# A decode step in which the sample group's local-attention caches are loaded two sequences at a time, 128 rows each

## The chip, the cores and the metric

The kernel runs on one core of one Trainium2 chip. Its engines work from queues of their own: TensorE (PE, with its weight loads PEld), VectorE (DVE), ScalarE (ACT), GpSimd (POOL) and SyncE (SP), which here only issues DMAs. The metric is the device time of one execution in microseconds (us), as the median of several runs. A result within 0.2% of the time before, about 5 us, counts as no change.

## What is computed

One layer of a hybrid decoder for a prompt group (one sequence of 256 tokens) and a sample group (8 sequences, one new token each) that share the weights: a half-step FFN, a mixer (gated DeltaNet beside sliding-window attention), cross-attention to a memory of 256 tokens, another half-step FFN, a final norm. The change lies in the sliding-window attention of the sample group:

```python
def swa_sample(q, k, v, sinks, k_buf, v_buf):        # k_buf, v_buf: (8, 128, 4, 64), oldest first
    kk = jnp.concatenate([k_buf, k], 1)              # 129 rows a sequence
    vv = jnp.concatenate([v_buf, v], 1)
    s = jnp.einsum('bthgd,bkhd->bhgtk', qg, kk) * (D ** -0.5)
    rel = (jnp.arange(T)[:, None] + wb) - jnp.arange(wb + T)[None, :]
    s = jnp.where((rel >= 0) & (rel < WINDOW), s, -jnp.inf)
    p = sink_softmax(s, sinks)
    o = jnp.einsum('bhgtk,bkhd->bthgd', p, vv)
    return o, kk[:, -wb:], vv[:, -wb:]
```

With a window of 128 and 128 cached rows, row 0 (the oldest) is masked out, so that 128 rows count: cache rows 1 to 127 and the new token. The order of these rows among themselves changes no sum, as long as keys and values have the same order. Each sequence has 4 key heads of 64, so that a row is 256 floats, 1 KB. All is in 32-bit floats.

## The kernel before

Nearly all of the time are large matrix products. `gemm` streams a weight matrix in pieces of 512 floats x 256 columns (`raw`, 512 KB, four buffers, loaded on SP at L152), splits each on ACT (`wh`, L155) and DVE (`wl`, L156) into two parts, and multiplies by 264 columns (256 prompt tokens and 8 sample tokens) in three products per 128 x 128 block (L183 to L185). Rows with `mm` or `mx` as output are these products. All smaller work runs in between.

The program is written in stages (the function `mixer`, printed below), and a scheduler then orders each engine's instructions by a simulated time, so that the stages overlap. `c0` to `c3` are pairs of DeltaNet heads (outputs `gd`), `s` projects keys, values and queries for the sliding window, `w0` to `w3` are the prompt's attention and `x` is the sample group's (outputs `sw`). The gate products (L900) fill TensorE meanwhile; their results go to DRAM from POOL (`gd<-gt`, L904), through two buffers.

In the stage `x` (`swa_sample`, written as a loop over 8 sequences) a sequence's keys come into a buffer `kc` by two DMAs on SP: rows 1 to 127 of its cache (L850), and the new key from the tile `kn` as row 127 (L851). TensorE transposes the block (L854), ACT copies it from PSUM (`kcT`, L856), and TensorE multiplies it by the queries (`qb`, L858). After a softmax the values come in the same way (L882, and L883 from `vn`) and are multiplied at L886. `kc` has two buffers for the keys and values of all sequences.

SP issues in order: a DMA that waits for its buffer, or that is slow to be issued, holds back the weight pieces and the state loads (`T`, `U`, `bv`, `d`, L658) behind it. At L682 TensorE multiplies the DeltaNet states by 2 columns, 32 instructions in a row per pair of heads. At L739 the rotary embedding swaps half-heads by DMAs on SP (`cth<-cy`).

Of the kernel before, what the change touches and what calls it, by code (L numbers as in the profile page):

```python
# [6 lines left out]
F32 = mybir.dt.float32  # L7
# [8 lines left out]
P = 128  # L16
# [3 lines left out]
NS = 8  # L20
# [49 lines left out]
class Build:  # L70
# [652 lines left out]
    def swa_proj(self, win, xs):  # L723
        nc, mc, o, i = self.nc, self.mc, self.o, self.i
        idn = self.K(C_ID)
        TT = nc.vector.tensor_tensor
        self.qr = mc.tile([P, 8, TOK], F32, name="qr")
        self.kd = {}
        self.Vt = mc.tile([P, 2, 256], F32, name="Vt")
        self.vn = mc.tile([NS, 256], F32, name="vn")  # L730
        self.kn = mc.tile([NS, 256], F32, name="kn")
        kt = mc.tile([P, 256], F32, name="kt")

        def rope_in(ps):
            y = self.gp.tile([P, TOK], F32, name="cy", bufs=2)
            TT(out=y, in0=ps, in1=self.norm.finish(), op=ALU.mult)
            t = mc.tile([P, TOK], F32, name="cth", bufs=2)
            for r in range(0, P, 32):
                nc.sync.dma_start(out=t[r:r + 32], in_=y[r ^ 32:(r ^ 32) + 32])  # L739
            TT(out=t, in0=t, in1=self.K(C_SN, TOK), op=ALU.mult)  # L740
            TT(out=y, in0=y, in1=self.K(C_CS, TOK), op=ALU.mult)
            return y, t

        def ev_k(j, ps):
            y, t = rope_in(ps)
            for par in range(2):
                g = 2 * j + par
                kd = mc.tile([P, TOK], F32, name=f"kd{g}")
                src = slice(64 * par, 64 * par + 64)
                for half in range(2):  # L750
                    TT(out=kd[64 * half:64 * half + 64], in0=y[src], in1=t[src], op=ALU.add)
                self.kd[g] = kd
                pt = self.evt()
                nc.tensor.transpose(pt[:, 0:64], kd[0:64, P:NP], idn[0:64, 0:64])
                nc.tensor.transpose(pt[0:NS, 64:128], kd[0:64, NP:TOK], idn[0:64, 0:64])
                nc.scalar.copy(out=kt[:, g * 64:(g + 1) * 64], in_=pt[:, 0:64])
                nc.scalar.copy(out=self.kn[:, g * 64:(g + 1) * 64], in_=pt[0:NS, 64:128])

        def ev_v(j, ps):
            y = self.gp.tile([P, TOK], F32, name="cy", bufs=2)  # L760
            TT(out=y, in0=ps, in1=self.norm.finish(), op=ALU.mult)
            pt = self.evt()
            nc.tensor.transpose(pt[:, 0:P], y[:, 0:P], idn)
            nc.tensor.transpose(pt[:, P:2 * P], y[:, P:NP], idn)
            nc.tensor.transpose(pt[0:NS, 256:384], y[:, NP:TOK], idn)
            nc.scalar.copy(out=self.Vt[:, :, j * P:(j + 1) * P], in_=pt[:, 0:256].rearrange("p (a b) -> p a b", a=2))
            nc.scalar.copy(out=self.vn[:, j * P:(j + 1) * P], in_=pt[0:NS, 256:384])

        def ev_q(c, ps):
            y, t = rope_in(ps)  # L770
            TT(out=self.qr[:, c], in0=y, in1=t, op=ALU.add)

        self.gemm(win, OFF_K, 256, xs, ev_k)
        self.gemm(win, OFF_V, 256, xs, ev_v)
        nc.gpsimd.dma_start(out=o["k_p"][0, 0].rearrange("t g d -> t (g d)"), in_=kt)
        ins = nc.gpsimd.dma_start(out=o["v_p"][0, 0].rearrange("t g d -> t (g d)"), in_=self.Vt[:, 1, :])
        with self.tc.issue_after(ins.ins):
            for nm, src, new in (("k_s", "cache_swa_k", self.kn), ("v_s", "cache_swa_v", self.vn)):
                nc.gpsimd.dma_start(out=o[nm][0, :, 0:P - 1], in_=i[src][0, :, 1:P])
                nc.gpsimd.dma_start(out=o[nm][0, :, P - 1].rearrange("b g d -> b (g d)"), in_=new)  # L780
            nc.gpsimd.dma_start(out=o["conv_s"][0, :, 0:2, :], in_=i["state_conv"][0, :, 1:3, :])
        for t0 in range(0, 8, 2):
            self.gemm(win, OFF_Q + t0 * P, 256, xs, lambda j, ps, t0=t0: ev_q(t0 + j, ps))

    def swt(self):
        return self.sw.tile([P, 512], F32, name="sw")
# [47 lines left out]
    def swa_sample(self):  # L834
        nc, mc, i, o = self.nc, self.mc, self.i, self.o
        idn = self.K(C_ID)
        TT = nc.vector.tensor_tensor
        sc = slice(NP, TOK)
        half = lambda q: slice(64 * q, 64 * q + 64)
        qb = mc.tile([P, NS, 2, 8], F32, name="qb")  # L840
        nc.vector.memset(qb, 0.0)
        for par in range(2):
            for jp in range(2):
                dst = qb.rearrange("p b t (r jj q) -> p r q t jj b", r=2, q=2)[half(par), par, jp]
                src = self.qr.rearrange("p (t r jj) x -> p r t jj x", t=2, r=2)[half(jp), par][:, :, :, sc]
                nc.vector.tensor_copy(out=dst, in_=src)
        ps = self.swt()
        for b in range(NS):
            kc = mc.tile([P, 256], F32, name="kc", bufs=2)
            nc.sync.dma_start(out=kc[0:P - 1], in_=i["cache_swa_k"][0, b, 1:P].rearrange("t g d -> t (g d)"))  # L850
            nc.sync.dma_start(out=kc[P - 1:P], in_=self.kn[b:b + 1, :])  # L851
            pt = self.swt()
            for t in range(2):
                nc.tensor.transpose(pt[:, t * P:(t + 1) * P], kc[:, t * P:(t + 1) * P], idn)  # L854
            kT = mc.tile([P, 2, P], F32, name="kcT", bufs=2)
            nc.scalar.copy(out=kT, in_=pt[:, 0:256].rearrange("p (a b) -> p a b", a=2))  # L856
            for t in range(2):
                nc.tensor.matmul(ps[:, b * 16 + t * 8:b * 16 + t * 8 + 8], kT[:, t], qb[:, b, t], start=True, stop=True)  # L858
        s1 = mc.tile([P, P], F32, name="s1")
        nc.vector.tensor_copy(out=s1, in_=ps[:, 0:P])  # L860
        pt = self.swt()
        nc.tensor.transpose(pt[:, 0:P], s1, idn)
        st = lambda name: mc.tile([P, 1], F32, name=name)
        m, se, sm = st("ssm"), st("sse"), st("ssu")
        nc.vector.tensor_reduce(out=m, in_=pt[:, 0:P], axis=AX.X, op=ALU.max)
        nc.vector.scalar_tensor_tensor(out=m, in0=m, scalar=0.125, in1=self.sinkc, op0=ALU.mult, op1=ALU.max)
        TT(out=se, in0=self.sinkc, in1=m, op=ALU.subtract)
        nc.vector.tensor_scalar(out=m, in0=m, scalar1=-1.0, scalar2=None, op0=ALU.mult)
        nc.scalar.activation(out=se, in_=se, func=AF.Exp)
        p = mc.tile([P, P], F32, name="s1")  # L870
        nc.scalar.activation(out=p, in_=pt[:, 0:P], func=AF.Exp, scale=0.125, bias=m, accum_out=sm)
        TT(out=sm, in0=sm, in1=se, op=ALU.add)
        nc.vector.reciprocal(out=sm, in_=sm)
        nc.vector.tensor_scalar(out=p, in0=p, scalar1=sm, scalar2=None, op0=ALU.mult)
        pt = self.swt()
        nc.tensor.transpose(pt[:, 0:P], p, idn)
        pT = mc.tile([P, P], F32, name="s3")
        nc.scalar.copy(out=pT, in_=pt[:, 0:P])
        po = self.swt()
        for b in range(NS):  # L880
            vc = mc.tile([P, 256], F32, name="kc", bufs=2)
            nc.sync.dma_start(out=vc[0:P - 1], in_=i["cache_swa_v"][0, b, 1:P].rearrange("t g d -> t (g d)"))  # L882
            nc.sync.dma_start(out=vc[P - 1:P], in_=self.vn[b:b + 1, :])  # L883
            for t in range(2):
                n = b * 16 + t * 8
                nc.tensor.matmul(po[:, n:n + 8], vc[:, t * P:(t + 1) * P], pT[:, n:n + 8], start=True, stop=True)  # L886
        for par in range(2):
            for jp in range(2):
                dst = self.os.rearrange("p (t r jj) x -> p r t jj x", t=2, r=2)[half(jp), par][:, :, :, sc]
                src = po[:, 0:P].rearrange("p (b t r jj q) -> p r q t jj b", b=NS, t=2, r=2, q=2)[half(par), par, jp]  # L890
                nc.vector.tensor_copy(out=dst, in_=src)
# [369 lines left out]
```

## Time and profile before

| | |
|---|---|
| median of 3 runs | 2570.62 us (2567.1 to 2571.18) |
| profiled execution, first to last instruction | 2570.9 us |
| TensorE busy | 2507.5 us, 98% |
| VectorE, ScalarE, GpSimd busy | 59%, 43%, 6% |
| bytes over DMA | 456.16 MB, mean 177 GB/s |

The profile gives the span of one execution; what lies around it can't be seen in the median, which is 0.3 us below the span. TensorE is busy nearly throughout, so the places to look at are those where it waits, and those where its granted clock is below 1. The granted clock takes two levels, 1.2 and 2.4 GHz, which the profile gives as 0.5 and 1.

### The profile page before, as it was taken

The page shows a single profiled execution, that of the slowest core. Times are in us where ns is not written, and L with a number is a line of the kernel's source. Part 1 is how long each engine was busy: PE and PEld are TensorE (multiplying, and loading weights), DVE is VectorE, ACT ScalarE, POOL GpSimd, SP SyncE. Part 2 cuts the span into 40 slices and gives each one's busy share as a digit, 9 for nine tenths or more (in the row PEclk, how much of TensorE's full clock was granted, in tenths as well). Part 3 has the DMA queues.
Part 4 walks back from the last instruction along what each step waited for, and adds up shares of the span by engine and source line. Part 5 has one row for each costly group of instructions (what it writes and reads, how often), then busy time and mean ns, then how long its engine had stood idle before and what let it go on. Part 6 is the DMA issues. An engine that isn't in the chain of part 4 may idle for free.

```text
span 2570.9 us, 48618 instructions
## 1 busy us (share of the span) xinstructions
PE 2507.5 (98%) x20127; PEld 2464.5 (96%) x20127; DVE 1508.5 (59%) x2507; ACT 1110.3 (43%) x1667; POOL 151.0 (6%) x203
## 2 busy tenths in 40 slices
PE   8999999999999999999789999999999999999998
PEld 8999999999998999989779999979999999999997
DVE  6555544555556858685355667687655544555544
ACT  4444333444444443454335545436444433444443
POOL 3000000000001002020020320000000000000000
PEclk9999999999999999999779999999999999999999
DMA  6555556556555556554345776674555555555553
GB/s 193 180 180 181 177 181 185 181 181 181 177 180 174 157 161 207 152 157 122 117 127 151 222 245 201 203 268 152 181 181 181 174 180 187 181 179 182 173 176 129
DMA packets 438589, 456.16 MB, mean 177 GB/s; under 512 B 18140, under 2 KB 425360, under 8 KB 438312
## 3 DMA queue, kind: packets, MB, share of 16 engines
q1 hardware_dynamic: 429376, 427.26, 53.9%
q0 software_dynamic: 8656, 24.67, 2.9%
q8 instruction: 157, 2.57, 0.4%
q10 hardware_dynamic: 336, 1.12, 0.1%
q14 instruction: 64, 0.52, 0.1%
HBM read 438.92 MB, written 14.98 MB: 177 GB/s over the span
## 4 chain that ended last, share of the span: by engine, by line
PE 93%; DMA 3%; DVE 2%; SPq 1%; ACT 0%; issue 0%; DVEq 0%; ACTq 0%
PE mm L183 18%; PE mm L185 18%; PE mm L184 18%; PE mx L183 11%; PE mx L185 11%; PE mx L184 11%; DMA kc<-kn 1%; DMA kc<-vn 1%; PE gd L574 1%; PE gd L579 1%; PE sw L803 1%; PE gd L682 1%; DVE wl L156 1%; DMA raw<-in_w_in_dram 0%; PE mm L988 0%; PE mm L990 0%
## 5 line engine op out<-in xcount | busy, mean ns | idle before, releaser
L156 DVE TENSOR_TENSOR wl<-raw,wh 128x1024 fp32r<-128x1024 f32 (+1 forms) x796 | 959.9, 1206 | 827.4 <-ACT wh L155 822.2
L155 ACT CAST wh<-raw 128x1024 fp32r<-128x1024 f32 (+1 forms) x796 | 820.5, 1031 | 1246.6 <-PE mm L184 669.1
L183 PE MATMUL mm<-xh,wh 128*128 128x264 f32 x2688 | 783.0, 292 | 6.0 <-ACT wh L155 6.0
L185 PE MATMUL mm<-xh,wl 128*128 128x264 f32 x2688 | 779.4, 291 | 3.4 <-DVE wl L156 3.4
L184 PE MATMUL mm<-xl,wh 128*128 128x264 f32 x2688 | 778.5, 290 | 0.0
L183 PEld LDWEIGHTS mm<-xh,wh 128*128 128x128 f32 x2688 | 518.4, 193 | 10.0 <-ACT wh L155 6.2
L185 PEld LDWEIGHTS mm<-xh,wl 128*128 128x128 f32 x2688 | 516.8, 193 | 6.4 <-DVE wl L156 4.2
L184 PEld LDWEIGHTS mm<-xl,wh 128*128 128x128 f32 x2688 | 517.7, 193 | 1.9 <-issue 1.5
L183 PE MATMUL mx<-xh,wh 128*128 128x264 f32 x1424 | 405.2, 285 | 1.1 <-DVE xl L1210 1.1
L185 PE MATMUL mx<-xh,wl 128*128 128x264 f32 x1424 | 405.4, 285 | 0.0
L184 PE MATMUL mx<-xl,wh 128*128 128x264 f32 x1424 | 404.4, 284 | 0.0
L183 PEld LDWEIGHTS mx<-xh,wh 128*128 128x128 f32 x1424 | 268.7, 189 | 1.4 <-issue 1.3
L184 PEld LDWEIGHTS mx<-xl,wh 128*128 128x128 f32 x1424 | 268.2, 188 | 0.0
L185 PEld LDWEIGHTS mx<-xh,wl 128*128 128x128 f32 x1424 | 268.1, 188 | 0.0
L185 PE MATMUL mm<-hh,wl 128*128 128x264 f32 x748 | 212.7, 286 | 0.0
L183 PE MATMUL mm<-hh,wh 128*128 128x264 f32 x748 | 212.4, 284 | 0.0
L184 PE MATMUL mm<-hl,wh 128*128 128x264 f32 x748 | 212.3, 284 | 0.0
L185 PE MATMUL mx<-hh,wl 128*128 128x264 f32 x660 | 187.6, 285 | 0.0
L183 PE MATMUL mx<-hh,wh 128*128 128x264 f32 x660 | 187.5, 284 | 0.0
L184 PE MATMUL mx<-hl,wh 128*128 128x264 f32 x660 | 187.4, 284 | 0.0
L184 PEld LDWEIGHTS mm<-hl,wh 128*128 128x128 f32 x748 | 140.9, 188 | 0.0
L183 PEld LDWEIGHTS mm<-hh,wh 128*128 128x128 f32 x748 | 140.6, 188 | 0.0
(572 smaller groups left out, 3020.9 us busy)
## 6 DMA issues: line engine op xcount, KB each, us to landing
raw<-in_ffn_w_dram SPq DMA_DIRECT2D x512, 512.0 KB
raw<-in_w_in_dram SPq DMA_DIRECT2D x152, 512.0 KB
raw<-in_w_out_dram SPq DMA_DIRECT2D x32, 512.0 KB
raw<-in_ffn_w_dram SPq DMA_DIRECT2D x32, 256.0 KB
raw<-in_w_br_gdn_dram SPq DMA_DIRECT2D x16, 512.0 KB
raw<-in_w_br_swa_dram SPq DMA_DIRECT2D x16, 512.0 KB
gd<-gt POOLq DMA_DIRECT2D x32, 132.0 KB, 3.2
tg<-gd POOLq DMA_DIRECT2D x32, 132.0 KB, 4.2
```

Source lines behind the costliest of these rows:

```text
L155: nc.scalar.copy(out=H, in_=raw)
L156: nc.vector.tensor_tensor(out=L, in0=raw, in1=H.bitcast(F32), op=ALU.subtract)
L183: nc.tensor.matmul(acc, wh, xh, start=(kg + c == 0), stop=False)
L184: nc.tensor.matmul(acc, wh, xl, start=False, stop=False)
L185: nc.tensor.matmul(acc, wl, xh, start=False, stop=(kg + c == nk - 1))
L574: nc.tensor.matmul(pP[:, a], A[:, a], uh[a], start=True, stop=True)
L579: nc.tensor.matmul(pU[:, a], T[:, a], Pm[:, a], start=True, stop=True)
L682: nc.tensor.matmul(pk[:, m:m + 2], Ss[h * 2 + b // 4][:, b % 4], kq[:, h, b, :], start=True, stop=True)
L803: nc.tensor.matmul(ps[j % 2][:, a // 2], self.qr[half, 2 * g + j // 2, qs], self.kd[g][half, 0:W], start=True, stop=True)
```

## The change

The keys and values of the sample group are loaded as whole blocks of two sequences, 128 rows x 2 x 256 (four loads for keys, L857, and four for values, L891, instead of eight each), on SP as before. The new token takes the place of row 0 and no longer of row 127. For keys this happens after the transposition: the new keys are taken already transposed from `kd` into a small tile `knT` (four DVE copies), and a DVE copy per sequence writes column 0 of `kcT` (L864); there is no DMA for it. For values a DMA per sequence writes row 0 of the block from `vn`, now issued by POOL (L893) and no longer by SP. `kc` has three buffers of two sequences each, and the prompt's key tile `kt`, which goes out as a cache, takes the first turn of one of them; the softmax's `s1`, `p` and `pT` use turns of `kcT`'s buffers; `kn` and `vn` lie in one tile.

```diff
@@ -727,9 +727,9 @@
         self.qr = mc.tile([P, 8, TOK], F32, name="qr")
         self.kd = {}
         self.Vt = mc.tile([P, 2, 256], F32, name="Vt")
-        self.vn = mc.tile([NS, 256], F32, name="vn")
-        self.kn = mc.tile([NS, 256], F32, name="kn")
-        kt = mc.tile([P, 256], F32, name="kt")
+        kvn = mc.tile([40, 256], F32, name="kvn")
+        self.kn, self.vn = kvn[0:NS], kvn[32:32 + NS]
+        kt = self.kc_tile()[:, 0, :]
...
@@ -781,6 +781,9 @@
             nc.gpsimd.dma_start(out=o["conv_s"][0, :, 0:2, :], in_=i["state_conv"][0, :, 1:3, :])
         for t0 in range(0, 8, 2):
             self.gemm(win, OFF_Q + t0 * P, 256, xs, lambda j, ps, t0=t0: ev_q(t0 + j, ps))
+
+    def kc_tile(self):
+        return self.mc.tile([P, 2, 256], F32, name="kc", bufs=3)
 
     def swt(self):
         return self.sw.tile([P, 512], F32, name="sw")
@@ -844,19 +847,25 @@
                 dst = qb.rearrange("p b t (r jj q) -> p r q t jj b", r=2, q=2)[half(par), par, jp]
                 src = self.qr.rearrange("p (t r jj) x -> p r t jj x", t=2, r=2)[half(jp), par][:, :, :, sc]
                 nc.vector.tensor_copy(out=dst, in_=src)
+        knT = mc.tile([P, 2, NS], F32, name="knT")
+        for t in range(2):
+            for q in range(2):
+                nc.vector.tensor_copy(out=knT[half(q), t, :], in_=self.kd[2 * t + q][half(q), sc])
         ps = self.swt()
-        for b in range(NS):
-            kc = mc.tile([P, 256], F32, name="kc", bufs=2)
-            nc.sync.dma_start(out=kc[0:P - 1], in_=i["cache_swa_k"][0, b, 1:P].rearrange("t g d -> t (g d)"))
-            nc.sync.dma_start(out=kc[P - 1:P], in_=self.kn[b:b + 1, :])
-            pt = self.swt()
-            for t in range(2):
-                nc.tensor.transpose(pt[:, t * P:(t + 1) * P], kc[:, t * P:(t + 1) * P], idn)
-            kT = mc.tile([P, 2, P], F32, name="kcT", bufs=2)
-            nc.scalar.copy(out=kT, in_=pt[:, 0:256].rearrange("p (a b) -> p a b", a=2))
-            for t in range(2):
-                nc.tensor.matmul(ps[:, b * 16 + t * 8:b * 16 + t * 8 + 8], kT[:, t], qb[:, b, t], start=True, stop=True)
-        s1 = mc.tile([P, P], F32, name="s1")
+        for b2 in range(0, NS, 2):
+            kc = self.kc_tile()
+            nc.sync.dma_start(out=kc, in_=i["cache_swa_k"][0, b2:b2 + 2].rearrange("b t g d -> t b (g d)"))
+            for b in (b2, b2 + 1):
+                pt = self.swt()
+                for t in range(2):
+                    nc.tensor.transpose(pt[:, t * P:(t + 1) * P], kc[:, b - b2, t * P:(t + 1) * P], idn)
+                kT = mc.tile([P, 2, P], F32, name="kcT", bufs=2)
+                nc.scalar.copy(out=kT, in_=pt[:, 0:256].rearrange("p (a b) -> p a b", a=2))
+                nc.vector.tensor_copy(out=kT[:, :, 0], in_=knT[:, :, b])
+                for t in range(2):
+                    nc.tensor.matmul(ps[:, b * 16 + t * 8:b * 16 + t * 8 + 8], kT[:, t], qb[:, b, t], start=True, stop=True)
+        sp2 = mc.tile([P, 2, P], F32, name="kcT", bufs=2)
+        s1 = sp2[:, 0]
         nc.vector.tensor_copy(out=s1, in_=ps[:, 0:P])
         pt = self.swt()
         nc.tensor.transpose(pt[:, 0:P], s1, idn)
@@ -867,23 +876,25 @@
         TT(out=se, in0=self.sinkc, in1=m, op=ALU.subtract)
         nc.vector.tensor_scalar(out=m, in0=m, scalar1=-1.0, scalar2=None, op0=ALU.mult)
         nc.scalar.activation(out=se, in_=se, func=AF.Exp)
-        p = mc.tile([P, P], F32, name="s1")
+        p = sp2[:, 1]
         nc.scalar.activation(out=p, in_=pt[:, 0:P], func=AF.Exp, scale=0.125, bias=m, accum_out=sm)
         TT(out=sm, in0=sm, in1=se, op=ALU.add)
         nc.vector.reciprocal(out=sm, in_=sm)
         nc.vector.tensor_scalar(out=p, in0=p, scalar1=sm, scalar2=None, op0=ALU.mult)
         pt = self.swt()
         nc.tensor.transpose(pt[:, 0:P], p, idn)
-        pT = mc.tile([P, P], F32, name="s3")
+        pT = mc.tile([P, 2, P], F32, name="kcT", bufs=2)[:, 0]
         nc.scalar.copy(out=pT, in_=pt[:, 0:P])
         po = self.swt()
-        for b in range(NS):
-            vc = mc.tile([P, 256], F32, name="kc", bufs=2)
-            nc.sync.dma_start(out=vc[0:P - 1], in_=i["cache_swa_v"][0, b, 1:P].rearrange("t g d -> t (g d)"))
-            nc.sync.dma_start(out=vc[P - 1:P], in_=self.vn[b:b + 1, :])
-            for t in range(2):
-                n = b * 16 + t * 8
-                nc.tensor.matmul(po[:, n:n + 8], vc[:, t * P:(t + 1) * P], pT[:, n:n + 8], start=True, stop=True)
+        for b2 in range(0, NS, 2):
+            vc = self.kc_tile()
+            nc.sync.dma_start(out=vc, in_=i["cache_swa_v"][0, b2:b2 + 2].rearrange("b t g d -> t b (g d)"))
+            for b in (b2, b2 + 1):
+                nc.gpsimd.dma_start(out=vc[0:1, b - b2, :], in_=self.vn[b:b + 1, :])
+            for b in (b2, b2 + 1):
+                for t in range(2):
+                    n = b * 16 + t * 8
+                    nc.tensor.matmul(po[:, n:n + 8], vc[:, b - b2, t * P:(t + 1) * P], pT[:, n:n + 8], start=True, stop=True)
         for par in range(2):
             for jp in range(2):
                 dst = self.os.rearrange("p (t r jj) x -> p r t jj x", t=2, r=2)[half(jp), par][:, :, :, sc]
```

The order shifts in the mixer only. In the stage `x` SP has these rows before, from the key loads of the fifth sequence on (`kc_...` are the turns of the buffer, `kn` the new keys, `vn` the new values, `raw_...` weight pieces):

```order
L850 DMA kc_14440<-in_cache_swa_k_dram 127x256
L851 DMA kc_14440<-kn_11284 1x16x16
L152 DMA raw_15390<-in_w_in_dram 128x4x256
L658 DMA T_13043<-in_state_gdn_dram 128x4x128
L850 DMA kc_14450<-in_cache_swa_k_dram 127x256
L851 DMA kc_14450<-kn_11284 1x16x16
L152 DMA raw_15434<-in_w_in_dram 128x4x256
L850 DMA kc_14460<-in_cache_swa_k_dram 127x256
L851 DMA kc_14460<-kn_11284 1x16x16
L152 DMA raw_15464<-in_w_in_dram 128x4x256
```

In the same place, from one weight piece before on, SP has now the last pair of keys and the first two pairs of values:

```order
L152 DMA raw_15347<-in_w_in_dram 128x4x256
L857 DMA kc_14458<-in_cache_swa_k_dram 128x2x256
L152 DMA raw_15377<-in_w_in_dram 128x4x256
L658 DMA T_13042<-in_state_gdn_dram 128x4x128
L891 DMA kc_14497<-in_cache_swa_v_dram 128x2x256
L152 DMA raw_15421<-in_w_in_dram 128x4x256
L891 DMA kc_14505<-in_cache_swa_v_dram 128x2x256
L152 DMA raw_15451<-in_w_in_dram 128x4x256
```

The first three pairs of keys are issued earlier, in the stage `s`, and the one-row DMAs are gone from SP.

At the start of the mixer SP had two of the loads of 127 rows among the first weight pieces, long before their use:

```order
L152 DMA raw_9108<-in_w_in_dram 128x4x128
L152 DMA raw_9282<-in_w_in_dram 128x4x256
L152 DMA raw_9312<-in_w_in_dram 128x4x256
L850 DMA kc_14400<-in_cache_swa_k_dram 127x256
L850 DMA kc_14410<-in_cache_swa_k_dram 127x256
L152 DMA raw_9342<-in_w_in_dram 128x4x256
```

Now only weight pieces stand there, and the first three pairs of keys come after the first rotary swap (`cth`) of the stage `s`, the third of them in the turn after that of `kt`:

```order
L739 DMA cth_11434<-cy_11432 32x264 x4
L152 DMA raw_11664<-in_w_in_dram 128x4x256
L658 DMA T_10147<-in_state_gdn_dram 128x4x128
L857 DMA kc_14404<-in_cache_swa_k_dram 128x2x256
L152 DMA raw_11694<-in_w_in_dram 128x4x256
L857 DMA kc_14422<-in_cache_swa_k_dram 128x2x256
L152 DMA raw_11746<-in_w_in_dram 128x4x256
L152 DMA raw_11776<-in_w_in_dram 128x4x256
L658 DMA U_10149<-in_state_gdn_dram 128x4x128
L658 DMA bv_10151<-in_state_gdn_dram 128x4x128
L152 DMA raw_11806<-in_w_in_dram 128x4x256
L857 DMA kc_14440<-in_cache_swa_k_dram 128x2x256
```

On POOL, before, the gate stores of the stage `x` stand like this:

```order
L904 DMA gd0_5_15162<-gt_15160 128x264
L904 DMA gd0_6_15290<-gt_15288 128x264
L904 DMA gd0_7_15296<-gt_15294 128x264
L626 DMA out_gdn_p_dram<-S_12984 128x2x128
L904 DMA gd0_8_15424<-gt_15422 128x264
L904 DMA gd0_9_15430<-gt_15428 128x264
L701 DMA ud2_13114<-sut_13112 16x128
```

Now the new values' rows stand among them, two per pair of sequences:

```order
L915 DMA gd0_5_15149<-gt_15147 128x264
L893 DMA kc_14497<-kvn_11283 1x16x16 x2
L915 DMA gd0_6_15277<-gt_15275 128x264
L893 DMA kc_14505<-kvn_11283 1x16x16 x2
L915 DMA gd0_7_15283<-gt_15281 128x264
L626 DMA out_gdn_p_dram<-S_12983 128x2x128
L893 DMA kc_14513<-kvn_11283 1x16x16 x2
L915 DMA gd0_8_15411<-gt_15409 128x264
L915 DMA gd0_9_15417<-gt_15415 128x264
L893 DMA kc_14521<-kvn_11283 1x16x16 x2
L701 DMA ud2_13113<-sut_13111 16x128
```

Each of these waits for the load of its pair. On TensorE the value products, which before stood in seven places between gate products, are now twelve rows in a row (the first three pairs of sequences) right behind the 32 state products of L682, then 13 gate products and some small work, and then the last pair.

## Rows read from the trace of the kernel before

**Rows 1.** The page, part 2: granted TensorE clock in 40 slices, in tenths.

```profile
PEclk9999999999999999999779999999999999999999
```

**Rows 2.** The page, part 4: the chain that ended last, by line, share of the span.

```profile
PE mm L183 18%; PE mm L185 18%; PE mm L184 18%; PE mx L183 11%; PE mx L185 11%; PE mx L184 11%; DMA kc<-kn 1%; DMA kc<-vn 1%; PE gd L574 1%; PE gd L579 1%; PE sw L803 1%; PE gd L682 1%; DVE wl L156 1%; DMA raw<-in_w_in_dram 0%; PE mm L988 0%; PE mm L990 0%
```

**Rows 3.** TensorE's waits, 800 to 1480 us: us in total, times, longest us.

```profile
PE sw L886 <- DMA kc<-vn: 14.5, 5, 5.1
PE sw L854 <- DMA kc<-kn: 11.1, 5, 3.2
PE mm L183 <- ACT wh L155: 6.6, 2, 6.0
```

**Rows 4.** Windows: us, busy us (instructions) of PE, PEld, DVE, ACT, POOL; PEclk, DMA share, GB/s.

```profile
1170.00:1206.80 36.80, 36.80 (x304) 34.41 (x302) 17.90 (x36) 16.23 (x33) 1.74 (x4) 1.00 0.42 123
...
1206.80:1333.50 126.70, 100.48 (x647) 95.82 (x646) 52.09 (x149) 40.44 (x90) 17.75 (x22) 0.76 0.39 118
...
1222.28:1228.00 5.72, 5.72 (x29) 5.72 (x30) 0.00 (x0) 0.51 (x2) 0.00 (x0) 0.55 0.54 153
1235.20:1240.90 5.70, 5.69 (x27) 5.70 (x28) 1.66 (x2) 2.11 (x4) 0.54 (x1) 0.50 0.38 117
1249.40:1254.40 5.00, 4.97 (x23) 5.00 (x24) 1.50 (x4) 1.42 (x2) 0.00 (x0) 0.50 0.40 122
1271.70:1291.90 20.20, 14.25 (x65) 13.29 (x65) 6.64 (x30) 3.67 (x10) 0.57 (x2) 0.59 0.14 47
1299.10:1322.70 23.60, 17.32 (x76) 15.31 (x75) 7.28 (x22) 3.38 (x5) 7.04 (x8) 0.50 0.47 143
813.30:817.50 4.20, 4.18 (x17) 3.88 (x18) 3.28 (x5) 3.35 (x4) 0.00 (x0) 0.50 0.46 143
```

**Rows 5.** Timeline of SP: start us, us, queue, line, operation, out<-in, count.

```profile
795.44 4.07 SPq L850 DMA_DIRECT2D kc<-in_cache_swa_k_dram  x2
...
1210.72 0.40 SPq L850 DMA_DIRECT2D kc<-in_cache_swa_k_dram  x1
1211.17 5.55 SPq L851 DMA_DIRECT2D kc<-kn  x1
```

**Rows 6.** DMA, 1213 to 1233 us: GB/s in 40 slices; an issue and its size.

```profile
GB/s 185 19 25 23 25 25 23 25 26 25 23 25 25 25 25 23 25 25 23 27 59 111 274 383 368 325 123 27 23 25 23 22 24 25 26 102 203 375 352 72
...
kc<-in_cache_swa_k_dram SPq DMA_DIRECT2D x3, 127.0 KB
```

**Rows 7.** Timeline of TensorE, two neighbours before a wait, two after.

```profile
1217.72 0.28 PE L184 MATMUL mm<-xl,wh 128*128 128x264 f32 x1
1217.84 0.28 PE L185 MATMUL mm<-xh,wl 128*128 128x264 f32 x1
...
1223.62 0.42 PE L184 MATMUL mm<-xl,wh 128*128 128x264 f32 x1
1223.84 0.42 PE L185 MATMUL mm<-xh,wl 128*128 128x264 f32 x1
```

**Rows 8.** Timeline of TensorE, state products and first value products; 8 instructions a row.

```profile
1268.17 1.02 PE L682 MATMUL gd<-kq,d 128*128 128x2 f32 x8 [0.61 <-DMA d<-in_state_gdn_dram]
1269.05 1.03 PE L682 MATMUL gd<-kq,T 128*128 128x2 f32 x8
...
1271.73 1.81 PE L886 MATMUL sw<-s,kc 128*128 128x8 f32 x8
```

**Rows 9.** The chain that ended last, in order of time: start us, us, what.

```profile
1211.17 10.97 DMA kc<-kn
...
1262.87 5.17 DMA d<-in_state_gdn_dram
```

**Rows 10.** Timeline of POOL [idle before].

```profile
954.21 0.59 POOL L775 DMA_DIRECT2D out_k_p_dram<-kt  x1 [43.02 <-ACT kn L757]
```

**Rows 11.** DMA issues of the whole span: count, KB each, us to landing.

```profile
out_conv_p_dram<-cs POOLq DMA_DIRECT2D x12, 3.0 KB, 1.6
```

**Rows 12.** Timeline of DVE, a small copy.

```profile
1263.64 0.16 DVE L674 COPY sdq<-gd 128x16 f32<-128x16 f32 x1
```

## The prediction, made before the changed kernel ran

> **What bounds the kernel now.** I read the page first. TensorE is busy in 98% of the span, but its granted clock falls in two of the 40 slices, at about 1221 to 1350 us [rows 1]; and the chain that ended last, otherwise matrix products, holds two DMAs, the one-row copies from `kn` and `vn`, with 1% of 2570.9 us each, more than any single small group on TensorE [rows 2]. So I asked for TensorE's waits in the mixer: 14.5 us in 5 waits for `vn` rows, 11.1 us in 5 for `kn` rows, and 6.6 us in 2 for `wh`, one of them of 6.0 us [rows 3]. The first two belong to the stage `x`, 1207 to 1313 us. The third, at 807 us, I put down to the same DMAs: SP issued two key loads at 795.4 us, which kept it for 4.07 us, among the first weight pieces [rows 5], and the piece behind them came late.
>
> Why do these loads take so long? In the stage `x` the DMAs move some 25 GB/s for most of the time, between bursts of up to 383 GB/s [rows 6]. 25 is about one sixteenth of 383: while a load of 127 rows runs, one engine of 16 seems to work, and the weight pieces behind it wait. The 127 KB of one load are 130,048 bytes, at 25 GB/s 5.2 us. That is about what SP spends on the row copy issued next, 5.55 us, after 0.40 us for the load itself [rows 5], and the copy lands 10.97 us after its issue began [rows 9]. Sixteen loads are 83 us on one engine, within a stage of 106 us. This, and not the volume (2 MB), is the bottleneck there.
>
> The waits cost twice. Before one of them, neighbouring products start 0.12 us apart, after it 0.22 us [rows 7]: the clock has gone from 2.4 to 1.2 GHz after TensorE stood idle for about 3 us. Each microsecond that TensorE is busy at the lower level is a loss of (0.22 - 0.12) / 0.22 = 0.45 us.
>
> **The change, part by part.**
>
> *Loads.* The 16 loads of 127 rows go; 8 of 128 x 2 rows come. With 128 partitions, like the weight pieces, they should run on all engines: 256 KB at 383 GB/s is 0.7 us, and one such load, `d` at 1262.87 us, took 5.17 us in all with a slow load before it [rows 9], while a 3 KB store lands in 1.6 us [rows 11]. I bound a load by 1.6 and 5.2 us. All three gains follow from it:
>
> - idle time: 11.1 + 14.5 + 6.0 = 31.6 us [rows 3].
> - clock: five stretches after waits in the stage `x` show 5.72, 5.69, 4.97, 14.25 and 17.32 us of busy TensorE at clocks of 0.55, 0.50, 0.50, 0.59 and 0.50 [rows 4]. The share at the lower level is twice what is missing to 1 (0.9, 1, 1, 0.82, 1), which makes 5.1 + 5.7 + 5.0 + 11.7 + 17.3 = 44.8 us, and 0.45 of it is 20.2 us.
> - the same at 813 us: 4.2 us [rows 4], lost 1.9 us.
>
> That is 53.7 us. What is late next: at 807 us the piece would be issued at 795.4 instead of 799.6 us, and with 5.2 us it lands at 800.6 us, before TensorE needs it. The first three key pairs come at about 940 to 960 us; the third waits for the store of `kt`, which POOL issued at 954.21 us [rows 10] and which lands 1.6 to 5.4 us later (the upper end is the rest of the one-row copy after its issue, 10.97 - 5.55). SP stood at that time for `kn` rows already, so I take 0; if cover is gone, weight pieces come up to 3.6 us late. The fourth key pair's buffer comes free with the second sequence's transposition, 104 rows of TensorE's order before the use; at 304 rows in 36.8 us [rows 4] these are 12.6 us, more than 5.2.
>
> *Rows.* The key rows go altogether. The value rows move to POOL, behind the load that they overwrite. POOL takes 0.59 us for an issue [rows 10], a landing 1.6 us [rows 11] to 5.4 us as above. Load and two rows cost 0.4 + 1.6 + 1.2 + 1.6 = 4.8 us to 0.4 + 5.2 + 1.2 + 5.4 = 12.2 us. For the first three pairs at least 124 rows of TensorE's order (15 us) lie between the free buffer and the use: hidden. What is queued behind the rows on POOL are gate stores (`gd_6` to `gd_9`), which have two buffers, and the DeltaNet row `ud` and come from products that TensorE does about as late as the keys and values of the stage; I let nobody wait for them. The last pair has less cover: its buffer comes free with the first 8 of 24 value products, and 16 products, 7 small instructions and 13 gate products follow. At the lower clock each takes 0.22 us (a value product 1.81 / 8 [rows 8]), so that the cover is 36 x 0.22 = 7.9 us. The wait is 0 to 4.3 us; I take 1.0, nearer to the lower end, since the row of 5.4 us ran behind a slow load.
>
> The Trainium skill, DMA: Bandwidth & Descriptors, section "Anatomy of one DMA — SWDGE (gpsimd) path", speaks against moving rows to GpSimd: there each DMA costs about 2.0 us plus its bytes at 436 GB/s, however small, and here two follow one another. As an estimate from this page the last pair takes 0.4 + 2.6 + 1.2 + 2.0 = 6.2 us, still under 7.9, so that its sum would be 1.0 us lower than mine. No row shows such a copy on POOL; the 1.6 us store agrees roughly.
>
> *What stays.* The clock falls without any wait too: the 32 products of L682 have 2 columns, and the value products right behind them start 0.22 us apart, where L682's start 0.88 / 8 = 0.11 us apart [rows 8]. Now 24 value products of 8 columns stand there in one piece. I let the lower level last until the 13 gate products are through: (24 + 7 + 13) x 0.22 = 9.7 us, of which 0.45 is 4.4 us that are not won back.
>
> *Small copies.* DVE gets 12, at 0.16 us [rows 12] 1.9 us, hidden, since DVE is half idle; 8 of them stand between ACT's copy and the key products, covered by some 15 gate products each. If cover is gone, 8 x 0.16 = 1.3 us. I take 0.5.
>
> *Sum.* 53.7 - 1.0 - 4.4 - 0.5 = 47.8 us. The profiled span is 2570.9 us, 0.3 above the median, so I predict 2523 us. As a check: from 1206.8 to 1333.5 us TensorE does 647 instructions in 126.7 us [rows 4]; at the rate before that, 8.26 per us, they would take 78 us, 48 less, to which the start of the mixer adds 7.9 and from which what stays goes off.
>
> **The rivals.**
>
> *The waiting moves to the last value pair.* With a free buffer only after the first pair's products, load and rows at their upper bounds, and TensorE at the full clock (cover 36 x 0.12 = 4.3 us), the wait is 7.9 us, 6.9 above mine, and the clock stays low as it did from 1299.1 us on, 0.45 x 17.32 = 7.8 us more. That gives 2523 + 14.7 = 2538 us. For it: the third buffer is shared by keys and values. Against it: the bounds come from DMAs behind a one-engine load.
>
> *The loads stay slow.* If blocks of 128 x 2 rows ran at 25 GB/s as well, a pair would take 10.5 us, 84 us for eight against 83 before, and three of them would stand before weight pieces at 945 us: about 2571 us, no change. For it: no load of this shape is in the trace. Against it: `T` and the weight pieces, with 128 partitions, run in the bursts of 383 GB/s [rows 6]. The Trainium skill, same page, section "Why a DMA increments its semaphore by 16 and not by 1", has a rule: a copy takes the largest number of engines up to 16 that divides its slowest dimension, which is 1 for 127 and 16 for 128. It agrees with the 25 GB/s, and leaves this rival little.
>
> *Slower: the value rows on POOL, one after the other.* If each of the 8 rows kept POOL as long as `kn` rows took, 10.97 us [rows 9], the six of the first three pairs need 65.8 us. Between the first pair's buffer and the value products lie 214 rows of TensorE's order, 25.9 us, less 5.6 for the load: TensorE waits 45.5 us, and for the last pair 5.6 + 21.9 - 7.9 = 19.6 us. With 53.7 - 4.4 won this is 2570.9 - 49.3 + 65.1 = 2587 us. It decides from 9.0 us per row on, where 8 rows less 22.6 us of cover make 49.3. Against it: the slow rows stood behind slow loads, and POOL issues a DMA in 0.59 us [rows 10].
>
> **How the numbers follow.** Forecast 0.77, waiting at the last pair 0.15, loads slow 0.05, slower 0.03. The forecast's own range: without what stays it is 2517, a few us of small products at the lower clock that my stretches leave out make 2514; the upper bounds of the wait, the copies and SP's delay add 3.3 + 0.8 + 3.6, which is 2531. To take in the first rival up to its price I go to 2538. A measurement can tell 0.2%, about 5 us, from no change. Faster gets the first two cases, 0.92, and a little of the third: 0.93. The same 0.03, slower 0.04.
>
> **What would show it.** After: no wait for `kn` or `kc` at the keys, no wait of `wh` at 807 us; loads of L857 and L891 without a stretch at 25 GB/s; SP's rows of the stage without issues of 5 us; one stretch at the lower clock of some 10 us after L682, with at most a few us of waiting for the last `vn` row; DVE, ACT and the stages after the mixer as before. It would be wrong if TensorE waited for value rows of the first three pairs, if a weight piece came late at 945 to 1000 us, or if the clock fell for other reasons in the stage `x`.

## The result, and the profile after

The changed kernel takes 2524.87 us (median of 4 runs, 2523.32 to 2526.39); the kernel before, on the same chip, took 2570.9 us (2567.1 to 2575.39). The ratio is 0.9821, with a 95% interval of 0.9809 to 0.9833. The forecast was 2523 us, in a range of 2514 to 2538. The profiled execution has a span of 2521.5 us, against 2570.9 before: 49.4 us less, where the sum said 47.8. Between the medians it is 46.0. The two profiled executions lie apart from their medians on opposite sides: the changed kernel's took 2523.32 us, the least of its four, 1.8 us more than its span. If the same 1.8 us go on top of the span before, that execution took 2572.7 us, 1.8 above its median; this is an estimate. The 0.3 us that were read ahead of the run, between the median and the span, therefore compared different executions.

The page of the changed kernel, part 2 (granted clock in 40 slices) and part 4 (the chain by line):

```profile
PEclk9999999999999999999899999999999999999999
...
PE mm L183 18%; PE mm L185 18%; PE mm L184 18%; PE mx L183 11%; PE mx L185 11%; PE mx L184 11%; PE gd L574 1%; PE gd L579 1%; PE gd L682 1%; PE sw L806 1%; PE mm L999 0%; DVE wl L156 0%; PE mm L1001 0%; PE mm L1000 0%; PE gd L584 0%; PE ap L235 0%
```

The two slices at 0.7 are gone; one at 0.8 stays [rows 1]. The two row copies have left the chain, and no DMA stands among its lines in their place [rows 2].

TensorE's waits in the changed kernel, 750 to 1440 us (us in total, times, longest us):

```profile
PE gd L540 <- DVE kb L531: 6.3, 3, 2.5
PE mm L185 <- DVE wl L156: 1.4, 1, 1.4
PE mm L183 <- ACT wh L155: 0.6, 1, 0.6
```

None of the three waits of [rows 3] is left but 0.6 us of `wh`. The wait for `kb` was there before, with 4.9 us in 2 waits; a third, of 1.4 us at 1272 us, is new.

Where the 49.4 us come from is seen by cutting both traces at the same instructions: from 750 us to the start of `ba` (L387), from the first key transposition to the state products of `c2` (L682), and from these to those of `c3`. First the kernel before (us, then busy us and instructions of PE, PEld, DVE, ACT, POOL, then clock, DMA share, GB/s):

```profile
750.00:821.86 71.86, 65.85 (x521) 65.12 (x520) 38.80 (x65) 28.85 (x40) 7.63 (x15) 0.95 0.58 176
...
1206.80:1268.17 61.37, 49.65 (x358) 48.64 (x356) 22.26 (x58) 18.98 (x35) 3.44 (x6) 0.83 0.42 128
1268.17:1424.94 156.77, 142.27 (x1043) 134.09 (x1044) 81.53 (x205) 64.92 (x141) 21.00 (x28) 0.87 0.44 131
```

and the changed kernel:

```profile
750.00:813.55 63.55, 63.55 (x522) 63.17 (x521) 39.46 (x69) 29.07 (x41) 8.14 (x16) 1.00 0.66 199
...
1198.74:1240.39 41.65, 41.65 (x358) 41.14 (x357) 22.44 (x64) 18.78 (x35) 6.55 (x12) 1.00 0.62 185
1240.39:1374.80 134.41, 133.00 (x1037) 126.30 (x1036) 83.76 (x210) 65.86 (x141) 22.73 (x30) 0.95 0.52 150
```

The three stretches give 8.3, 19.7 and 22.4 us, together 50.4; the rest of the program gives 1.0 us back (0.2 before the keys, 0.7 behind `c3`). Within a stretch, the time less the busy time is what TensorE stood idle: 6.0 + 11.7 + 14.5 = 32.2 us before, 1.4 us after, so 30.8 us won. The busy time fell by 2.3 + 8.0 + 9.3 = 19.6 us for nearly the same instructions: that is the clock. In the key stretch, 358 instructions run at 1.00 where they ran at 0.83.

SP and then POOL in the changed kernel (start us, us, queue, line, operation, out<-in, count):

```profile
935.06 0.50 SPq L857 DMA_DIRECT2D kc<-in_cache_swa_k_dram  x1
...
1202.91 0.37 SPq L857 DMA_DIRECT2D kc<-in_cache_swa_k_dram  x1
...
1210.21 0.37 SPq L891 DMA_DIRECT2D kc<-in_cache_swa_v_dram  x1
...
1246.87 0.37 SPq L891 DMA_DIRECT2D kc<-in_cache_swa_v_dram  x1
```

```profile
1213.87 1.01 POOL L893 DMA_DIRECT2D kc<-kvn  x2 [12.09 <-PE sw L861]
...
1250.18 0.99 POOL L893 DMA_DIRECT2D kc<-kvn  x2 [12.52 <-DMA kc<-in_cache_swa_v_dram]
```

Each load keeps SP for 0.4 to 0.5 us, and no issue behind one lasts 5 us as in [rows 5]. The DMA issues of the whole span (count, KB each, median us to landing) give the prices that had to be bounded:

```profile
kc<-in_cache_swa_k_dram SPq DMA_DIRECT2D x4, 256.0 KB, 4.2
kc<-in_cache_swa_v_dram SPq DMA_DIRECT2D x4, 256.0 KB, 2.8
...
kc<-kvn POOLq DMA_DIRECT2D x8, 1.0 KB, 2.5
```

A load takes 2.8 to 4.2 us (bounds 1.6 and 5.2), a row copy 2.5 us (bounds 1.6 and 5.4). The GB/s of the changed kernel from 1207 to 1247 us, in 40 slices, have no run of slices at 25, as [rows 6] has:

```profile
GB/s 45 313 166 60 289 293 322 69 18 0 31 262 351 295 198 348 166 342 127 125 271 9 155 351 30 218 303 1 71 344 172 300 200 363 132 105 347 72 0 0
```

Last, TensorE after the state products of `c2`:

```profile
1242.10 1.32 PE L682 MATMUL gd<-kq,U 128*128 128x2 f32 x8
1243.28 1.85 PE L682 MATMUL gd<-kq,bv 128*128 128x2 f32 x8
1244.98 5.27 PE L897 MATMUL sw<-kcT,kc 128*128 128x8 f32 x24
1250.10 0.37 PE L697 MATMUL gd<-idn,su 128*16 128x128 f32 x1
...
1254.79 0.42 PE L184 MATMUL mm<-xl,wh 128*128 128x264 f32 x1
1255.01 0.43 PE L897 MATMUL sw<-kcT,kc 128*128 128x8 f32 x2
```

and its window, in the columns of the stretches above:

```profile
1243.28:1254.79 11.51, 11.51 (x53) 11.05 (x53) 4.03 (x24) 3.35 (x10) 1.47 (x3) 0.50 0.22 71
```

The 24 value products start 0.22 us apart, and so do the gate products behind them, until about 1255 us. This window holds only the part that lies at 0.50 throughout; the clock falls within the products before it (eight take 1.32 us, then 1.85) and comes back at about 1256 us. The last pair is used at 1255.01 us without a wait, 8.1 us after its load was issued.

### The profile page after: what moved, and what is told of

It is laid out like the page before. It is cut to its first block, busy times and chain, and to the rows that moved or that the text cites. A ratio compares the mean times of both kernels' runs of the same rounds, so it can differ in the third digit from the quotient of the medians.

```text
span 2521.5 us, 48602 instructions
## 1 busy us (share of the span) xinstructions
PE 2491.5 (99%) x20127; PEld 2450.3 (97%) x20127; DVE 1511.8 (60%) x2519; ACT 1111.3 (44%) x1667; POOL 156.1 (6%) x211
## 4 chain that ended last, share of the span: by engine, by line
PE 96%; DVE 2%; ACT 0%; issue 0%; DMA 0%; SPq 0%; DVEq 0%; ACTq 0%
PE mm L183 18%; PE mm L185 18%; PE mm L184 18%; PE mx L183 11%; PE mx L185 11%; PE mx L184 11%; PE gd L574 1%; PE gd L579 1%; PE gd L682 1%; PE sw L806 1%; PE mm L999 0%; DVE wl L156 0%; PE mm L1001 0%; PE mm L1000 0%; PE gd L584 0%; PE ap L235 0%
## 5 line engine op out<-in xcount | busy, mean ns | idle before, releaser
L183 PEld LDWEIGHTS mm<-xh,wh 128*128 128x128 f32 x2688 | 511.8, 190 | 2.9 <-issue 1.8
L185 PEld LDWEIGHTS mm<-xh,wl 128*128 128x128 f32 x2688 | 510.1, 190 | 4.1 <-DVE wl L156 1.8
L184 PEld LDWEIGHTS mm<-xl,wh 128*128 128x128 f32 x2688 | 511.3, 190 | 2.0 <-issue 1.7
```

Source lines behind the costliest of these rows:

```text
L183: nc.tensor.matmul(acc, wh, xh, start=(kg + c == 0), stop=False)
L184: nc.tensor.matmul(acc, wh, xl, start=False, stop=False)
L185: nc.tensor.matmul(acc, wl, xh, start=False, stop=(kg + c == nk - 1))
```

## The experiments

The theory was that the shape of the load is the whole effect: 127 rows run on one DMA engine, and with it the weight pieces and row copies behind it are late. A row of the kernel before bears on the one engine: while a load of 127 rows runs, the 16 DMA engines are busy for 0.07 of the time on average, where one of 16 alone would make 0.06 (columns as in [rows 4]).

```profile
1215.00:1218.00 3.00, 2.49 (x20) 2.42 (x20) 0.00 (x0) 0.37 (x1) 0.00 (x0) 1.00 0.07 25
```

The rivals were the number of DMAs on SP (16 loads and 16 rows become 8 loads), the path of the row copies, and the third buffer. Each run stands beside runs of the kernel before on the same chip.

**One edit to the kernel before: the load in two parts of 112 and 15 rows.** Everything else stays, so SP issues 16 DMAs more.

```diff
-            nc.sync.dma_start(out=kc[0:P - 1], in_=i["cache_swa_k"][0, b, 1:P]...)
+            for r0, r1 in ((0, 112), (112, P - 1)):
+                nc.sync.dma_start(out=kc[r0:r1], in_=i["cache_swa_k"][0, b, 1 + r0:1 + r1]...)
```

(The values likewise.) 

> The kernel before, with each load of 127 rows issued as two, 112 and 15 rows, into the same place; one sequence at a time, two buffers and the one-row copies on SP stay. Theory A (a load of 127 rows runs on one DMA engine at 25 GB/s and holds everything behind it): nearly all of the 46 us come back, less what short waits for two buffers leave: 2526 to 2545 us, no stretch at 25 GB/s, SP's row copies issued in 0.5 to 1 us instead of 5, no wait at 807 us. Rival B (the one-row copies on SP's queue are what costs): 2560 us or more, since they all stay. Rival C (fewer and earlier loads, three buffers): also 2560 us or more.

Measured: 2521.3 us, ratio 0.9795 (0.978 to 0.981), below the 2526 to 2545 that I expected: I had allowed for waits for the two buffers. Of TensorE's waits for the caches one line is left, with 1.0 us:

```profile
PE sw L888 <- DMA kc<-vn: 1.0, 2, 0.8
```

So two buffers, one sequence per block and rows from SP are all good enough; the rows per load alone bring all that the change brings, as far as the intervals can tell. 16 more DMAs on SP did no harm that shows.

**126 rows and 1.** The same edit, with 126 in place of 112.

> The kernel before, each 127-row load as 126 rows and 1 row. Theory (the number of engines is the largest number up to 16 that divides the rows: 14 for 126): a load of 126 KB takes about 0.4 us at fourteen sixteenths of 383 GB/s, no stretch at 25 GB/s, 2519 to 2526 us like the split in 112 and 15. Rival (only row counts that 16 divides run on many engines): a stretch at 25 to 50 GB/s stays and the time is 2560 to 2573 us.

Measured: 2520.16 us, ratio 0.9798 (0.9782 to 0.9815). The GB/s of 1207 to 1247 us in 40 slices:

```profile
GB/s 130 30 237 291 215 190 222 288 103 0 66 213 380 170 236 352 224 314 233 197 0 81 319 124 22 211 287 46 207 320 256 253 177 297 80 215 277 0 0 83
```

One row less in the load, and the stretches at 25 GB/s of [rows 6] are gone. The rival, that only row counts which 16 divides are good, falls.

**113 rows and 14.** The same edit with 113, a prime number like 127.

> The kernel before, each 127-row load as 113 rows (a prime number) and 14 rows. Theory (largest divisor up to 16: 1 for 113): the long piece still runs on one engine, 113 KB at 25 GB/s or 4.6 us instead of 5.2, the waits shrink by a tenth to a third, 2555 to 2570 us. Rival (two shorter loads instead of one are what helps, whatever their rows): 2520 to 2530 us.

Measured: 2562.18 us, ratio 0.9969 (0.9958 to 0.9979). Its GB/s in the same stretch, then TensorE's waits from 750 to 1480 us, then SP:

```profile
GB/s 267 11 30 147 163 357 60 24 38 25 25 24 25 27 36 97 339 334 63 23 24 38 116 346 128 125 25 54 101 313 180 121 25 38 29 198 323 38 145 22
```

```profile
PE sw L888 <- DMA kc<-vn: 11.4, 4, 4.0
PE sw L855 <- DMA kc<-kn: 10.2, 5, 3.1
PE mm L183 <- ACT wh L155: 5.2, 2, 4.6
```

```profile
1210.73 4.51 SPq L851 DMA_DIRECT2D kc<-in_cache_swa_k_dram  x2
1215.29 0.52 SPq L852 DMA_DIRECT2D kc<-kn  x1
```

This kernel has as many DMAs as the other two splits and 42 us more than the one with 126. 24 to 25 GB/s is back, and the waits fall only by about a sixth (32.2 us in [rows 3], 26.8 here), within the tenth to a third that was expected for a load that is a ninth shorter. SP is again held at the DMA behind the long one, here the 14 rows, for 4.4 to 5.2 us. Splitting as such is worth little: 0.3%.

**The changed kernel with 127 rows in its blocks.** Buffers, number of DMAs and their order stay; the oldest row is left out of the load (key row 0 is set to zero on DVE instead).

```diff
-            nc.sync.dma_start(out=kc, in_=i["cache_swa_k"][0, b2:b2 + 2]...)
+            nc.vector.memset(kc[0:1], 0.0)
+            nc.sync.dma_start(out=kc[1:P], in_=i["cache_swa_k"][0, b2:b2 + 2, 1:P]...)
```

> The changed kernel, with blocks of 127 rows of two sequences (row 0 isn't loaded; for keys it is set to zero, for values the new row comes as in the changed kernel). Everything else of the change stays: half as many loads, three buffers, no row copy on SP. Theory A: a pair takes 10.5 us on one engine; three pairs hold the weight pieces at 935 to 975 us and five hold them in the stage x: 2550 to 2590 us. Rival C (fewer, earlier loads and the third buffer bring the gain): 2525 to 2532 us. Rival B (no row copies on SP): the same 2525 to 2532 us.

Measured: 2597.59 us, ratio 1.0091 (1.0074 to 1.0108): 73 us above the changed kernel (measured on another chip), for one row of 128, and slower than the kernel before; I had put it at 2550 to 2590, so it costs more than I expected. The GB/s from 936 to 959 us in 40 slices, TensorE's longest waits, and SP among the weight pieces:

```profile
GB/s 116 329 388 152 231 146 0 0 21 25 25 23 23 23 21 23 50 23 21 23 91 310 379 355 34 21 23 21 28 18 25 23 23 23 21 23 21 23 21 23
```

```profile
PE mm L183 <- ACT wh L155: 30.2, 4, 14.8
PE gd L682 <- DMA d<-in_state_gdn_dram: 13.2, 2, 12.8
PE sw L898 <- DMA kc<-in_cache_swa_v_dram: 7.7, 1, 7.7
```

```profile
936.76 0.40 SPq L858 DMA_DIRECT2D kc<-in_cache_swa_k_dram  x1
938.01 8.92 SPq L152 DMA_DIRECT2D raw<-in_w_in_dram  x1
946.98 1.45 SPq L858 DMA_DIRECT2D kc<-in_cache_swa_k_dram  x1
948.53 19.76 SPq L152 DMA_DIRECT2D raw<-in_w_in_dram  x2
```

TensorE waits 7.7 us for the caches, which three buffers of two sequences fetch early, and 43.4 us for the weight pieces and states behind them. So the changed kernel's larger blocks and third buffer are no gain of their own: without the shape they move the harm to where it costs more. This is the answer to the rival of the buffers.

**Only the first two key loads split** (112 and 15 rows `if b < 2`), to price the wait at 807 us by itself.

> The kernel before, with only the first two key loads (those at the start of the mixer, 795 us) split into 112 and 15 rows. Theory A: the wait of 6.0 us at 807 us and the low clock behind it go, 8 us: 2563 us, with the waits of the stage x as before. Rival (the weight piece at 807 us is late for another reason, as the constants that POOL loads there): no change, 2571 us, and the wait stands.

Measured: 2562.56 us, ratio 0.9955 (0.994 to 0.997), 9.1 us less than the kernel before beside it (2571.69), where the prediction had priced this place at 6.0 + 1.9 = 7.9. The waits of the stage `x` stay:

```profile
PE sw L887 <- DMA kc<-vn: 14.9, 5, 5.7
PE sw L855 <- DMA kc<-kn: 12.3, 5, 3.3
...
PE mm L183 <- ACT wh L155: 0.6, 1, 0.6
```

The wait of 6.0 us is gone. That late weight piece was due to two cache loads that would be needed 400 us later, as read from [rows 5].

**Only the row copies on POOL**, in the kernel before (`nc.sync` becomes `nc.gpsimd` at L851 and L883).

> The kernel before, with the 16 one-row copies issued by POOL instead of SP; the loads of 127 rows stay. Theory A: the one engine is busy for 83 us as before, so the waits stay for the most part: 2558 to 2580 us, stretches at 25 GB/s as before. Rival B (SP held for 5 us by each row copy): 2525 to 2540 us.

Measured: 2567.97 us, ratio 0.9982 (0.9971 to 0.9994), which is within the 0.2% that count as no change (by its interval the gain is 0.06 to 0.29%). The waits take another name:

```profile
PE sw L886 <- DMA kc<-in_cache_swa_v_dram: 11.9, 4, 5.4
PE sw L854 <- DMA kc<-in_cache_swa_k_dram: 10.3, 5, 3.9
PE mm L183 <- ACT wh L155: 6.0, 1, 6.0
```

The chain before named the copies from `kn` and `vn` [rows 2]; they were only the last to land, held up by the load. Their path was worth 3.7 us at the median, not the 46.

**Is the changed kernel behind the bare split?** 2524.87 against 2521.3 us raised the question. My theory was that its 24 value products in one piece, at the low clock, cost the 3.6 us. Two variants of the changed kernel, the kernel itself and the split in 112 and 15 ran on one chip: `nc.gpsimd` back to `nc.sync` at L893, and `bufs=3` to `bufs=2` at L786, after which the scheduler puts 16 value products in the first piece, not 24 (the expectation counts them in pairs: 8, 1 and 7).

> The changed kernel, with the value token rows copied from SyncE's queue again instead of GpSimd's. Theory (the shape of the loads is the whole effect, and the changed kernel loses 3 to 4 us against the split loads because its 24 value products stand in one piece, which ends at half clock): 2523 to 2527 us, as the changed kernel, since the products still stand in large pieces and no row copy waits for a 5-us load any more. Rival 1 (the loss comes from the row copies on GpSimd): 2520 to 2522 us. Rival 2 (rows behind the loads on SP hold the later weight pieces): 2530 us or more, with a wait on wh or wl of several us.

> The changed kernel with two cache buffers instead of three; its value products then stand as 8 and later 1 and 7 and not in one piece at the end. Theory (the loss against the split loads is the piece of value products at half clock and what follows it): 2521 to 2523 us, with a shorter stretch of 0.22-us neighbours after the softmax's transpose than the changed kernel's 10 us. Rival (the third buffer is what keeps the waits away): a wait on a key or value pair of 3 us or more comes back and the time is 2527 to 2535 us.

> The changed kernel itself, beside the others on one chip. Both theories: 2523 to 2527 us, ratio 0.981 to 0.983; it is here so that the difference to the split loads is taken on one chip.

> The kernel before with each 127-row load as 112 and 15 rows, beside the changed kernel. Theory (the shape of the loads brings all, the rest of the change costs 3 to 4 us): 2520 to 2523 us and an interval of the ratio that does not touch the changed kernel's. Rival (the two differ by the chip alone): intervals that overlap.

| | median us | ratio | 95% interval |
|---|---|---|---|
| value rows on SP | 2521.56 | 0.9810 | 0.9794 to 0.9826 |
| two buffers | 2523.18 | 0.9812 | 0.9798 to 0.9827 |
| the changed kernel again | 2523.99 | 0.9822 | 0.9803 to 0.9841 |
| 112 and 15 rows again | 2522.27 | 0.9819 | 0.9802 to 0.9836 |

All four intervals overlap: the difference is not there to be explained, and none of these kernels can be said to beat the changed one. My expectations did not hold in all: the rows on SP came out at 2521.56 us and not at 2523 to 2527, two buffers at 2523.18, just above 2521 to 2523, and the split's interval touches the changed kernel's; none of this is clear of the noise. Two rivals fall in the traces: with the rows on SP TensorE waits only 0.6 us for `wh` and 1.8 for `wl`, and with two buffers it waits for no cache load.

The theory on the 24 products can't be told from chance. The split in 126 and 1 has 8 value products behind L682 and not 24:

```profile
1242.84 1.85 PE L682 MATMUL gd<-kq,bv 128*128 128x2 f32 x8
1244.55 1.85 PE L888 MATMUL sw<-s,kc 128*128 128x8 f32 x8
```

Here are 20 us from the start of this L682 on, first in the changed kernel, then in its second trace, then in the split in 126 and 1:

```profile
1240.39:1260.39 20.00, 20.00 (x118) 19.40 (x117) 10.96 (x42) 7.35 (x20) 5.43 (x7) 0.66 0.37 112
...
1240.20:1260.20 20.00, 20.00 (x144) 19.40 (x143) 13.39 (x55) 9.53 (x27) 7.55 (x9) 0.83 0.43 130
...
1239.80:1259.80 20.00, 20.00 (x127) 19.26 (x126) 10.91 (x48) 10.09 (x31) 2.02 (x3) 0.74 0.44 126
```

By the missing share (twice 0.34, 0.17 and 0.26 of 20 us) the lower level lasts about 13.6, 6.8 and 10.4 us. The changed kernel alone, with the same 24 products in the same place, has both the longest and the shortest of these. At 0.45 us lost per us, the 6.8 us between its two traces are 3.1 us, about as much as the difference that was to be explained (their spans are 2521.5 and 2518.9 us).

## Why the prediction was right

- **The cause.** One DMA engine for 127 rows, read from 25 against 383 GB/s, is borne out by the busy share of 0.07, and the part of the row count is shown by three edits: 126 and 1 (fast) beside 113 and 14 (slow), which differ in nothing but the rows, and 128 to 127 in the changed kernel (slow). The Trainium skill, DMA: Bandwidth & Descriptors, section "Why a DMA increments its semaphore by 16 and not by 1", gives the rule of the largest divisor up to 16. The rates seen here agree with it: stretches around 25 GB/s (mostly 21 to 28) with 127 and 113 rows, none with 112, 126 and 128. The runs alone don't settle the rule for other counts: both slow counts are odd primes and all three fast ones are even, and no load of, say, 125 rows was tried.
- **Idle time.** Predicted 31.6 us won less 1.0 at the last value pair and 0.5 for DVE's copies, that is 30.1; measured 30.8. Neither deduction was needed: load, rows and landing of the last pair fit into 8.1 us, where the cover had been worked out as 7.9, and TensorE stands idle nowhere in the key stretch. In their place came 1.4 us for `kb`, a wait that DVE sets; why it is late was not looked into. So the sum comes near partly because these errors cancel.
- **Clock.** Predicted 20.2 + 1.9 - 4.4, that is 17.7; measured 19.6. This is the largest error, 1.9 us. The stretches at the lower level were listed only where they were plain.
- **What stays.** The low clock was put at 9.7 us from the first of the 24 value products to the last of the 13 gate products; that piece takes 9.8 us (1244.98 to 1254.79), all at 0.50. But some state products before it and about 1 us behind it are at the lower level too, 13.6 us in all, which at 0.45 is 6.1 us not won back instead of 4.4. That the size is near is luck as well: in the second trace of the same kernel the lower level lasts 6.8 us. The length doesn't follow from 24 products in one piece; what sets it is left open.
- **Row copies on POOL.** They take 0.5 us each to issue and 2.5 us to land (1.6 to 3.4), well within the bounds and far from the 9.0 us from which the slower rival decides. The Trainium skill, same page, section "Anatomy of one DMA — SWDGE (gpsimd) path", gives about 2.0 us; the trace has a quarter more at the median. The estimate from that page in the prediction also used its figures for GpSimd's path for the load, which SP issues: 2.6 us there, 2.8 in the trace.
- **Start of the mixer.** Predicted 6.0 + 1.9 = 7.9 us, measured 8.3 in the changed kernel. SP's delay by early key pairs, priced at 0 to 3.6 us, was 0: no weight piece came late there, and the state products of `c0` start 8.1 us earlier than before (969.9 against 978.0 us).
- **A slip that enters no sum.** The prediction sets sixteen loads, 83 us on one engine, against the 106 us of the stage `x`. Two of them ran at 795 us [rows 5], so that fourteen fall into the stage, 73 us.

Together: 30.1 + 17.7 = 47.8 us were predicted; 30.8 + 19.6 less the 1.0 that the rest of the program gives back are the 49.4 of the profile.

## What to carry to other kernels

Where a small load makes SP stand for microseconds at the next issue, look at its GB/s: here a flat stretch near a sixteenth of the peak went with a transfer on one engine, and adding or splitting off one row cured it. The wait was mostly not named after that load, but after a copy, a weight piece or a state queued behind it, so undo the shape before the copies, buffers or queues. Count the clock beside the idle time: here 30.8 us of waits brought another 19.6 us of busy time. And take a second trace before explaining 3 us: the same kernel had the low clock for 13.6 us in one execution and for 6.8 in another.

## What the hardware showed that I had not expected

A transfer on one engine can harm what is queued behind it more than its own reader: in the changed kernel with 127-row blocks TensorE waited 30.2 us for weights and 13.2 us for a state, and 7.7 us for the caches themselves. SP issued one weight piece in 8.92 us and two in 19.76 us there; what holds the issue can't be seen in the trace. An extra DMA on SP, by contrast, cost little here. In the split in 126 and 1, SP issues both loads of a sequence in 0.62 us and the row in 0.53, where one row copy kept it for 5.55 us in [rows 5]:

```profile
1202.30 0.62 SPq L851 DMA_DIRECT2D kc<-in_cache_swa_k_dram  x2
1202.96 0.53 SPq L852 DMA_DIRECT2D kc<-kn  x1
```
